# Block 2 of a two-block network on one Trainium2 core: the last twelve projections take their PSUM tiles from the buffers of the solve's and scan's tiles

## Chip, core and metric

The kernel runs on one core of a Trainium2 chip. The metric is the device time of one execution in microseconds, lower is better. TensorE (PE) multiplies matrices and writes its results to PSUM, a memory of eight banks; VectorE (DVE), ScalarE (ACT) and GpSimd (POOL) read them from there; SyncE (SP) issues most of the DMA transfers. TensorE's clock has two levels, 1.2 and 2.4 GHz, and the profile gives the granted share of the upper one (0.50 to 1.00).

## What is computed

The input is 512 tokens of width 1024. Block 1 is an RWKV-7 recurrence beside a neighbourhood attention, followed by a mixture of experts. Block 2, where the change lies, is a mixer of three branches and an MLP. All branches are fed by one projection of the normalised tokens:

```python
h = modulate(x, g, shift, scale)
z = h @ w_in
...
def gdn_chunk_scan(q, k, v, g, beta, s0):
    def step(s, xs):
        ...
        a = -jnp.einsum('bhid,bhjd->bhij', kb, kc) * jnp.exp(jnp.where(strict, diff, -jnp.inf))
        sol = lax.linalg.triangular_solve(eye - a, rhs, left_side=True, lower=True, unit_diagonal=True)
        w, u = sol[..., :dk], sol[..., dk:]
        v_new = u - w @ s
        o = (qc * jnp.exp(gcum)[..., None]) @ s + attn @ v_new
        s_new = jnp.exp(g_last)[..., None] * s + jnp.einsum('bhjd,bhje->bhde', kc * jnp.exp(g_last - gcum)[..., None], v_new)
        return s_new, o
```

Hyena takes a short convolution of its input (three taps) and then long convolutions; GLA and GDN gate their outputs with further columns of the projection. GDN has four heads, and runs forward and backward over the sequence.

## The kernel before

The program is written in Python as generators that emit instructions; a framework then orders the instructions of each engine by what they need, above all by when a buffer of a pool comes free. `weave` (L331) runs several generators together: it always advances the one whose emitted work divided by its weight is smallest.

**Projections.** `side_proj` (L1899) makes the 28 blocks of 128 columns that the mixer needs, one after the other. Each goes through `gemm_cm` (L297): a PSUM tile `gps` of 128x512, the weights loaded (`wraw`) and split into a rounded part `wh` on ScalarE (L287) and a rest `wl` on VectorE (L288), and 24 matmuls 128x512 in lines 293 to 295, eight steps of three products. What follows depends on the block: a short convolution (`conv`, L1277 and L1279) for the six `hy` blocks, tanh and a product (L1924, L1925) for the six `dg` and `gg` blocks. The result is stored to DRAM (L1926) for the later stages. The first 16 blocks are needed by GDN and GLA and are made by `early()` ahead of the branch of `gla_general` (L1689, L1690); the last twelve, `dg`/`gg` and `hy`, aren't needed until after the scan, and run beside `chain()`.

**The chain.** `chain()` solves two pairs of heads and then scans. `gdn_solve` (L1416) makes for each head the tiles `dps_` (L1427), `kkp` (L1437) and `qkp` (L1445), and calls `inverse` (L637) for the pair: 15 pairs of small steps on VectorE (L661, L662), a copy (L663) that goes to DRAM and back (`qd`, `qc`), a product on VectorE (L671, `qv`) and eight groups of products `ips` on TensorE (L682). `gdn_scan` (L1455) then goes through eight chunks. In each chunk the four heads have the small products `gxp` (L1467), `gup` (L1477), `gsp` (L1491) and `gop` (L1502, L1504), with steps on VectorE and ScalarE between them. The state runs from chunk to chunk.

**PSUM.** A tile of PSUM is taken by a tag, and each of the four tags `g`, `p`, `s` and `i` has two buffers. The projections run under a view that renames the tags:

```python
w = self.w = self.view(dict(p="g", s="g", i="p"), wg=512)
...
v = self.view({}, rib=2)
```

So a projection that asks for `g` gets `g`, and one that asked for `i` would get a buffer of `p`. The chain runs under `v`, which renames nothing: `dps_`, `kkp`, `qkp` and `gop` are on `p`, `gxp` and `gup` on `s`, `ips` and `gsp` on `i`. Before the change the projections thus have the two buffers of `g` for themselves. Tiles of one tag follow each other in the order in which the program asks for them: each waits until the readers of the tile two places earlier are done.

Of the kernel before, what the change touches and what calls it, by code (L numbers as in the profile page):

```python
# [19 lines left out]
T = 512  # L20
# [86 lines left out]
def w2_cols():  # L107

    r = {}
    ar = lambda a, n: np.arange(a, a + n)  # L110
    G, N = 768, 1952
    for hp in range(2):
        kv = np.concatenate([ar(N + 384 + 192 * hp, 192), ar(N + 768 + 192 * hp, 192)])
        for j in range(3):
            r[f"kv{hp}{j}"] = kv[128 * j:128 * j + 128]
    z = lambda n: np.full(n, -1)
    r["misc"] = np.concatenate([ar(N + 1536, 16), z(16), ar(G + 1152, 16), z(16), ar(G + 1168, 16), z(48)])
    for j in range(3):
        r[f"dq{j}"] = ar(N + 128 * j, 128)
    for hp in range(2):  # L120
        for nm, o in (("gk", 192), ("gq", 0)):
            r[f"{nm}{hp}"] = np.concatenate([ar(G + o + 96 * hp, 48), z(16), ar(G + o + 96 * hp + 48, 48), z(16)])
    for j in range(3):
        r[f"gv{j}"] = ar(G + 384 + 128 * j, 128)
        r[f"gg{j}"] = ar(G + 768 + 128 * j, 128)
        r[f"dg{j}"] = ar(N + 1152 + 128 * j, 128)
    for j in range(6):
        r[f"hy{j}"] = ar(128 * j, 128)
    return r
# [17 lines left out]
W2 = {n: i for i, n in enumerate(w2_cols())}  # L147
# [41 lines left out]
class K:  # L189
# [1709 lines left out]
    def side_proj(self, pool, later):  # L1899


        nc, A = self.nc, self.A
        cw = self.cp.tile([128, 6, 4], F32, name="hcw")
        nc.sync.dma_start(cw, A["hy_cw"])
        for n in SIDE_BLOCKS:
            self.we = nc.gpsimd if n in GDN_BLOCKS else nc.vector
            if n == "gk0":
                pool = later()
            ps = self.proj2(n, 128, T)
            if n in GDN_BLOCKS:  # L1910
                i = GDN_BLOCKS.index(n)
                y, d = self.conv_silu(pool, ps, 128, 8, 64, self.cw[:, (i + 6) % 9]), self.cvd[i]
            else:
                y = pool.tile([128, T], F32, name="sg", bufs=2)
                if n in self.gpd:
                    d = self.gpd[n]
                    nc.scalar.activation(y, ps, AF.Copy)
                elif n[:2] == "hy":
                    j = int(n[2])
                    d = self.hud[j]  # L1920
                    self.conv(pool, ps, 128, 8, 64, 3, cw[:, j], bias=cw[:, j, 3:4], out=y)
                else:
                    d = self.sgd[3 * (n[0] == "g") + int(n[2])]
                    nc.scalar.activation(y, ps, AF.Tanh, scale=0.5)  # L1924
                    nc.vector.scalar_tensor_tensor(y, y, 1.0, ps, op0=OP.add, op1=OP.mult)  # L1925
            nc.sync.dma_start(d, y)  # L1926
            self.there.add(n)
            yield 6
# [168 lines left out]
    def mixer_in(self):  # L2097

        nc, A, tc = self.nc, self.A, self.tc
        tp = tc.tile_pool  # L2100
        w, sp = self.w, self.w.sp

        def load(pool, d, tag):
            t = pool.tile([128, T], F32, name=tag, tag=tag, bufs=2)
            nc.sync.dma_start(t, d)
            return t

        with tp(name="mf", bufs=1) as mf:
            with tp(name="gd", bufs=1) as gd:
                w.misc(mf, 8)  # L2110
                v = self.view({}, rib=2)
                v.mfb = w.mfb

                st = {}
                w.there = set()
                def later():
                    w.spx.close()
                    return self.far.enter_context(tp(name="sp2", bufs=1, side="right"))
                side = w.side_proj(sp, later)

                def prep():
                    with tp(name="gt", bufs=1) as gt:
                        def src(n):
                            while n not in w.there:
                                next(side)
                            return load(gt, self.cvd[GDN_BLOCKS.index(n)], "yld")
                        st["g"] = v.gdn_gates(gd, v.mfb[:16], 8)
                        yield 10
                        st["q"] = yield from v.gdn_q(8, gd, gt, src)
                        for hp in range(2):  # L2130
                            st[hp] = yield from v.gdn_kv(hp, 8, gd, gt, src, hp)

                def early():
                    while not w.there.issuperset(SIDE_BLOCKS[:16]):
                        yield next(side)
                with tp(name="gf", bufs=1) as gf:
                    self.run(self.weave((early(), 96), (prep(), 60), (v.gla_flags(8, gf), 20)))
                with tp(name="gz", bufs=1) as ga:
                    v.gla_general(8, ga, lambda n: load(ga, self.gpd[n], "lsc"), self.oad)

                with tp(name="gs", bufs=1) as gs, tp(name="rp2", bufs=1) as v.rp:
                    heads = []

                    def chain():
                        with tp(name="gs2", bufs=1) as tmp, tp(name="ri2", bufs=1) as v.ri:
                            for hp in range(2):
                                kv, kT = st[hp]
                                E, TQ = yield from v.gdn_solve(hp, 8, gs, tmp, st["g"], kT, st["q"], hp)
                                heads.extend((2 * hp + e, kT[:, e], st["q"][:, 2 * hp + e], kv[:, :, e], kv[:, :, 2 + e], E[:, e], TQ[e])
                                             for e in range(2))  # L2150
                        yield from v.gdn_scan(8, gs, heads, st["g"], self.ogd)
                    next(side)
                    self.run(self.weave((chain(), 192), (side, 66)))
                    self.far.close()
                    self.oa = self.ox.enter_context(tp(name="oa", bufs=1, side="right")).tile([128, 8, 384], F32, name="oa")
                    nc.sync.dma_start(self.oa, self.oad.rearrange("c p d -> p c d"))
                    hp = self.far.enter_context(tp(name="hy", bufs=1, side="right"))
                    u = self.view(dict(p="g", s="g", i="g"))

                    def hyena():  # L2160
                        yield from u.hy_tables(hp)
                        yield from u.hyena(hp, 0)
                        yield from u.hyena(hp, 1)
            with tp(name="ga", bufs=1) as ga, tp(name="hn", bufs=1) as hn:
                un = self.view(dict(p="i"))
                self.run(self.weave((v.gla(8, False, ga, lambda n: load(ga, self.gpd[n], "lsc"), self.oa), 112),
                                    (un.head_norm_out(hn, self.ogd, 0, self.gng, 5), 36), (hyena(), 88)))
            self.far.close()
# [130 lines left out]
```

## Time and profile before

| | |
|---|---|
| runs | 2195.75, 2176.99, 2178.66 us; median 2178.66 |
| profiled execution | 2177.16 us, span 2175.4 us |
| mean granted clock | 0.932 |
| PE busy | 1954.9 us (90% of the span) |
| DVE busy | 1136.3 us (52%) |
| ACT busy | 719.2 us (33%) |
| POOL busy | 245.5 us (11%) |

All times inside the program are counted from the start of the span of the profiled execution. Matmuls are pipelined, so that the time from one's start to the next one's start is shorter than its own duration. Some matmul records are missing from a trace. A busy TensorE is not one at its peak: its granted clock says at which level it worked. The stretch that the change touches lies between 1390 and 1720 us: the last part of `early()`, the branch of `gla_general` (not taken), the solve with its two inverses, the scan, and the stage of Hyena and the gated norms behind it.

### The profile page before, as it was taken

The page shows a single profiled execution, that of the slowest core. Times are in us where ns is not written, and L with a number is a line of the kernel's source. Part 1 is how long each engine was busy: PE and PEld are TensorE (multiplying, and loading weights), DVE is VectorE, ACT ScalarE, POOL GpSimd, SP SyncE. Part 2 cuts the span into 40 slices and gives each one's busy share as a digit, 9 for nine tenths or more (in the row PEclk, how much of TensorE's full clock was granted, in tenths as well). Part 3 has the DMA queues.
Part 4 walks back from the last instruction along what each step waited for, and adds up shares of the span by engine and source line. Part 5 has one row for each costly group of instructions (what it writes and reads, how often), then busy time and mean ns, then how long its engine had stood idle before and what let it go on. Part 6 is the DMA issues. An engine that isn't in the chain of part 4 may idle for free. (4 is left out here: it accounts for less than half of the span.)

```text
span 2175.4 us, 37783 instructions
## 1 busy us (share of the span) xinstructions
PE 1954.9 (90%) x15280; PEld 1427.1 (66%) x15280; DVE 1136.3 (52%) x2542; ACT 719.2 (33%) x1390; POOL 245.5 (11%) x254
## 2 busy tenths in 40 slices
PE   7899999999698889988999487899999789999997
PEld 6676767666466764444524266677667577898897
DVE  4565645563362545455461487487456675434433
ACT  4333223333262433121322365422153234312321
POOL 0101011110100211111000031130002150010000
PEclk9999989999799989999999798999579899999999
DMA  6424232432854549979687433332152342333332
GB/s 160 145 61 131 82 102 65 126 111 75 183 175 158 165 133 322 327 262 328 244 300 251 181 116 103 104 81 80 44 171 62 127 144 76 97 93 93 97 92 74
DMA packets 177123, 312.21 MB, mean 144 GB/s; under 512 B 78648, under 2 KB 95816, under 8 KB 176938
## 3 DMA queue, kind: packets, MB, share of 16 engines
q1 hardware_dynamic: 167274, 291.84, 42.6%
q0 software_dynamic: 6784, 10.51, 1.7%
q10 hardware_dynamic: 2880, 7.34, 1.1%
q8 instruction: 123, 2.02, 0.4%
q14 instruction: 62, 0.51, 0.1%
HBM read 278.23 MB, written 39.77 MB: 146 GB/s over the span
## 5 line engine op out<-in xcount | busy, mean ns | idle before, releaser
L288 DVE TENSOR_TENSOR wl<-wraw,wh 128x1024 fp32r<-128x1024 f32 (+2 forms) x215 | 227.9, 1062 | 235.7 <-ACT wh L287 235.3
L287 ACT ACTIVATE wh<-wraw 128x512 fp32r<-128x512 f32 (+2 forms) x233 | 195.7, 844 | 251.7 <-PE gpt L326 136.9
L293 PE MATMUL gps<-hh,wh 128*128 128x512 f32 x568 | 235.2, 415 | 0.4 <-DVE kS L380 0.4
L294 PE MATMUL gps<-hh,wl 128*128 128x512 f32 x568 | 232.5, 410 | 1.2 <-DVE wl L288 1.2
L295 PE MATMUL gps<-hl,wh 128*128 128x512 f32 x568 | 233.0, 411 | 0.0
L1178 PE MATMUL hps<-w,xT 128*64 128x512 f32 x512 | 142.4, 611 | 3.3 <-DMA w<-in_w_moe 3.2
L324 PE MATMUL gpt<-wh,mh 128*128 128x256 f32 x512 | 142.9, 279 | 0.0
L325 PE MATMUL gpt<-wl,mh 128*128 128x256 f32 x512 | 142.9, 279 | 0.0
L326 PE MATMUL gpt<-wh,ml 128*128 128x256 f32 x512 | 142.9, 279 | 0.0
L293 PEld LDWEIGHTS gps<-hh,wh 128*128 128x128 f32 x568 | 108.2, 191 | 29.5 <-issue 2.9
L294 PEld LDWEIGHTS gps<-hh,wl 128*128 128x128 f32 x568 | 107.9, 190 | 29.5 <-DVE wl L288 4.2
L295 PEld LDWEIGHTS gps<-hl,wh 128*128 128x128 f32 x568 | 107.7, 190 | 25.7 <-issue 2.0
L293 PE MATMUL gps<-lhh,wh 128*128 128x512 f32 x232 | 98.0, 424 | 16.7 <-ACT wh L287 6.2
L294 PE MATMUL gps<-lhh,wl 128*128 128x512 f32 x232 | 96.2, 416 | 3.8 <-DVE wl L288 2.2
L324 PEld LDWEIGHTS gpt<-wh,mh 128*128 128x128 f32 x512 | 96.2, 188 | 0.1
L325 PEld LDWEIGHTS gpt<-wl,mh 128*128 128x128 f32 x512 | 96.2, 188 | 0.1
L326 PEld LDWEIGHTS gpt<-wh,ml 128*128 128x128 f32 x512 | 96.2, 188 | 0.0
L295 PE MATMUL gps<-lhl,wh 128*128 128x512 f32 x232 | 95.4, 413 | 0.0
L2003 POOL TENSOR_TENSOR x<-x,xev 128x512 f32<-128x512 f32 x36 | 50.2, 1403 | 388.3 <-DVE xev L2001 388.0
L1178 PEld LDWEIGHTS hps<-w,xT 128*64 128x64 f32 x512 | 36.9, 138 | 66.2 <-issue 50.8
L1279 DVE SCALAR_TENSOR_TENSOR cout<-cpad,cw,cout 128x512 f32<-128x512 f32 (+1 forms) x90 | 66.9, 743 | 2.1
L2019 DVE TENSOR_TENSOR uld<-uld 128x512 f32<-128x512 f32 x32 | 22.2, 693 | 87.3 <-ACT uld L2018 87.3
(1181 smaller groups left out, 4226.9 us busy)
## 6 DMA issues: line engine op xcount, KB each, us to landing
w<-in_w_moe SPq DMA_DIRECT2D x192, 512.0 KB
wraw<-in_w_modb SPq DMA_DIRECT2D x48, 512.0 KB
wraw<-in_w_in_2b SPq DMA_DIRECT2D x41, 512.0 KB
wraw<-in_w_mlp1b SPq DMA_DIRECT2D x32, 512.0 KB
wraw<-in_w_mlp2b SPq DMA_DIRECT2D x32, 512.0 KB
wraw<-in_w_inb SPq DMA_DIRECT2D x31, 512.0 KB
bm<-in_c_bias SPq DMA_DIRECT2D x16, 256.0 KB
wraw<-in_w_inb ACTq DMA_DIRECT2D x8, 512.0 KB
```

The source lines that it names most:

```text
L287: nc.scalar.activation(wh, raw[:, o:o + g], AF.Copy)
L288: self.we.tensor_sub(wl, raw[:, o:o + g], wh)
L293: nc.tensor.matmul(ps, wh, hh, start=first, stop=False)
L294: nc.tensor.matmul(ps, wl, hh, start=False, stop=False)
L295: nc.tensor.matmul(ps, wh, hl, start=False, stop=last)
L324: nc.tensor.matmul(ps, hh[:, g, sl], wh[:, k], start=f, stop=False, skip_group_check=True)
L325: nc.tensor.matmul(ps, hh[:, g, sl], wl[:, k], start=False, stop=False, skip_group_check=True)
L326: nc.tensor.matmul(ps, hl[:, g, sl], wh[:, k], start=False, stop=l, skip_group_check=True)
L1178: nc.tensor.matmul(ps[q], xT[:, 4 * kh + k, q], self.parts[h][:, 512 * (k - 2 * c):512 * (k - 2 * c) + 512], start=kh == 0 and k == 0, sto ...
L1279: nc.vector.scalar_tensor_tensor(ov[:n], pv[:n, :, j:j + L], wcol[:n, j:j + 1], ov[:n], op0=OP.mult, op1=OP.add)
L2003: (nc.gpsimd if last is None or cb < 3 else nc.vector).tensor_add(o, o, t)
L2019: nc.vector.tensor_mul(f, f, f)
```

## The change

The seventeenth and later projections take their PSUM tile by tag `i`, which the view makes `p`: the two buffers of `dps_`, `kkp`, `qkp` and `gop`. The seventeenth projection is no longer emitted ahead of the chain, and the weight of the projections in the weave is 72 instead of 66 (the chain's is 192).

```diff
@@ side_proj
-            ps = self.proj2(n, 128, T)
+            ps = self.gemm_cm("w_in_2b", W2.get(n, n), self.hh, self.hl, T, tag="i" if len(self.there) >= 16 else "g")
@@ mixer_in
-                    next(side)
-                    self.run(self.weave((chain(), 192), (side, 66)))
+                    self.run(self.weave((chain(), 192), (side, 72)))
```

The order of TensorE's instructions changes from the branch of `gla_general` to the end of the scan. Of the twelve projections, 33 matmuls stood ahead of the branch before and none do now. Between the branch and the first inverse's `ips` there were 107; now there are 114. Here is TensorE from the last groups of the first inverse on, before the change (`gps` is a projection, one number for each):

```order
L682 MATMUL ips_13819<-W_13798,Z_13722 64x64 x16
L295 MATMUL gps_14242<-lhl_11436,wh_14261 128x512
L293 MATMUL gps_14242<-lhh_11435,wh_14261 128x512
L294 MATMUL gps_14242<-lhh_11435,wl_14262 128x512
L295 MATMUL gps_14242<-lhl_11436,wh_14261 128x512
L1477 MATMUL gup_14281<-gX_14221,TQ0_13817 64x96 x2
L1477 MATMUL gup_14288<-gX_14227,TQ1_13836 64x96 x2
L1502 MATMUL gop_14338<-gS_7764,qT__12153 64x96 x2
L1502 MATMUL gop_14345<-gS_7764,qT__12153 64x96 x2
L293 MATMUL gps_14391<-lhh_11435,wh_14394 128x512
```

After that row 119 further matmuls of five projections follow before the second inverse's `ips`. The same place in the changed kernel:

```order
L1477 MATMUL gup_14249<-gX_14227,TQ1_13836 64x96 x2
L1502 MATMUL gop_14299<-gS_7764,qT__12153 64x96 x2
L1502 MATMUL gop_14306<-gS_7764,qT__12153 64x96 x2
L1504 MATMUL gop_14299<-vn__14247,E0_13421 64x96 x2
L1504 MATMUL gop_14306<-vn__14254,E0_13421 64x96 x2
L1502 MATMUL gop_14313<-gS_7764,qT__12153 64x96 x2
L1502 MATMUL gop_14320<-gS_7764,qT__12153 64x96 x2
L682 MATMUL ips_14025<-qv_14022,No_13970 64x64 x16
L682 MATMUL ips_14044<-qv_14022,No_13974 64x64 x16
```

The second inverse's products now follow the first chunk's groups at once: the next projection's tile shares `p` with the `gop` tiles of heads 2 and 3 (14313, 14320), which need the second inverse.

On VectorE, the small steps of the second inverse (`tmp16`, `q16`) before the change, with convolution (`sg`) and weight split (`wl`) between them:

```order
L662 TENSOR_REDUCE q16_14023<-tmp16_14024 128x8
L1277 TENSOR_SCALAR sg_14608<-cpad_14609,hcw_11604 128x512
L661 SCALAR_TENSOR_TENSOR tmp16_14024<-q16_14023,n16_14021 128x9x9
L1279 SCALAR_TENSOR_TENSOR sg_14608<-cpad_14609,hcw_11604,sg_14608 128x512
L662 TENSOR_REDUCE q16_14023<-tmp16_14024 128x9
L1279 SCALAR_TENSOR_TENSOR sg_14608<-cpad_14609,hcw_11604,sg_14608 128x512
L661 SCALAR_TENSOR_TENSOR tmp16_14024<-q16_14023,n16_14021 128x10x10
L288 TENSOR_TENSOR wl_14747<-wraw_14728,wh_14746 128x512
L662 TENSOR_REDUCE q16_14023<-tmp16_14024 128x10
L288 TENSOR_TENSOR wl_14885<-wraw_14882,wh_14884 128x512
```

And in the changed kernel:

```order
L662 TENSOR_REDUCE q16_13984<-tmp16_13985 128x8
L661 SCALAR_TENSOR_TENSOR tmp16_13985<-q16_13984,n16_13982 128x9x9
L662 TENSOR_REDUCE q16_13984<-tmp16_13985 128x9
L661 SCALAR_TENSOR_TENSOR tmp16_13985<-q16_13984,n16_13982 128x10x10
L662 TENSOR_REDUCE q16_13984<-tmp16_13985 128x10
L661 SCALAR_TENSOR_TENSOR tmp16_13985<-q16_13984,n16_13982 128x11x11
```

The 15 pairs of steps now follow one another with nothing between them; the convolutions and splits stand in the scan's chunks instead.

In the scan, TensorE before the change, in chunk 1 (the one projection there, `gps_15217`, is strung through chunks 0 to 3, and chunks 4 to 7 hold none):

```order
L293 MATMUL gps_15217<-lhh_11435,wh_15220 128x512
L1477 MATMUL gup_14435<-gX_14370,TQ0_13817 64x96 x2
L294 MATMUL gps_15217<-lhh_11435,wl_15221 128x512
L295 MATMUL gps_15217<-lhl_11436,wh_15220 128x512
L1477 MATMUL gup_14442<-gX_14376,TQ1_13836 64x96 x2
L1491 MATMUL gsp_14463<-vd__14438,kv0_12336 96x96
L1491 MATMUL gsp_14464<-vd__14438,kv0_12336 96x96
L1477 MATMUL gup_14449<-gX_14382,TQ2_14195 64x96 x2
```

And in the changed kernel, in chunk 4:

```order
L1467 MATMUL gxp_14847<-gSn_14752,kT1_12839 64x96 x2
L293 MATMUL gps_14909<-lhh_11435,wh_14912 128x512
L1477 MATMUL gup_14853<-gX_14832,TQ0_13817 64x96 x2
L294 MATMUL gps_14909<-lhh_11435,wl_14913 128x512
L295 MATMUL gps_14909<-lhl_11436,wh_14912 128x512
L1477 MATMUL gup_14860<-gX_14838,TQ1_13836 64x96 x2
L1491 MATMUL gsp_14881<-vd__14856,kv0_12336 96x96
L1491 MATMUL gsp_14882<-vd__14856,kv0_12336 96x96
L1477 MATMUL gup_14867<-gX_14844,TQ2_14195 64x96 x2
L293 MATMUL gps_14909<-lhh_11435,wh_14912 128x512
```

The scan now holds seven projections: one in chunk 1 (three single matmuls and a run of 21), one in chunk 2 as a run of 24, two in chunk 3 (a run of 24, and one strung out), and one in each of chunks 4, 5 and 6, strung out as here. Chunk 7 holds none.

## Rows read from the trace of the kernel before

**Rows 1.** Windows by stage: busy time and instructions of each engine, granted clock, DMA share.
```profile
1410.00:1505.50 95.50, 88.46 (x1057) 70.30 (x1059) 73.15 (x151) 23.07 (x42) 20.88 (x23) 0.98 0.35 90
1505.50:1599.00 93.50, 91.08 (x602) 58.14 (x600) 46.83 (x176) 19.55 (x61) 0.00 (x0) 0.59 0.14 46
```

**Rows 2.** Chain that ended last, in the scan: start, duration, what.
```profile
1557.34 1.00 PE gup L1477 x8
...
1558.92 0.51 PE gup L1477 x4
...
1568.97 1.00 PE gup L1477 x8
```

**Rows 3.** Timeline of PE in chunk 1 of the scan, at the full clock.
```profile
1512.63 0.49 PE L295 MATMUL gps<-lhl,wh 128*128 128x512 f32 x1
1513.05 0.39 PE L1467 MATMUL gxp<-gSn,kT 96*64 96x96 f32 x4
1513.37 0.50 PE L293 MATMUL gps<-lhh,wh 128*128 128x512 f32 x1
...
1514.26 0.39 PE L1467 MATMUL gxp<-gSn,kT 96*64 96x96 f32 x4
```

**Rows 4.** Windows, all engines; the third figure from the end is PE's clock.
```profile
1410.00:1413.00 3.00, 2.65 (x5) 1.49 (x5) 0.39 (x2) 0.63 (x1) 0.00 (x0) 0.50 0.03 8
1413.00:1418.00 5.00, 5.00 (x75) 3.92 (x75) 3.94 (x6) 0.60 (x1) 2.30 (x2) 0.93 0.00 2
1517.50:1522.00 4.50, 4.50 (x36) 3.04 (x36) 2.35 (x10) 1.24 (x5) 0.00 (x0) 1.00 0.02 4
1522.00:1526.00 4.00, 4.00 (x21) 2.48 (x23) 1.48 (x6) 0.34 (x1) 0.00 (x0) 0.62 0.13 49
1526.00:1588.00 62.00, 62.00 (x386) 39.70 (x384) 29.15 (x113) 12.44 (x39) 0.00 (x0) 0.50 0.12 39
```

**Rows 5.** Windows of the tile gps alone (PE, PEld, DVE, ACT), by stretch.
```profile
508.00:518.00 10.00, 6.42 (x18) 2.85 (x18) 0.00 (x0) 0.69 (x1) 1.00 0.15 39
1421.50:1427.20 5.70, 5.70 (x24) 4.42 (x24) 0.00 (x0) 0.00 (x0) 1.00 0.47 110
1461.00:1496.70 35.70, 30.41 (x124) 22.81 (x124) 0.68 (x1) 3.29 (x6) 1.00 0.47 119
1508.00:1522.00 14.00, 3.77 (x10) 1.53 (x9) 0.00 (x0) 0.00 (x0) 1.00 0.04 15
1526.00:1545.00 19.00, 5.25 (x8) 2.19 (x8) 0.00 (x0) 0.36 (x1) 0.50 0.00 1
```

**Rows 6.** Timeline of PE at the second inverse's products.
```profile
1496.72 2.08 PE L682 MATMUL ips<-qv,No 64*64 64x64 f32 x64 [0.40 <-DVE qv L671]
```

**Rows 7.** Timeline of PE around the branch.
```profile
1399.90 2.32 PE L1381 MATMUL tcp<-ct,kv 128*96 128x128 f32 x8 [1.06 <-DVE kv L1372]
...
1410.35 0.79 PE L293 MATMUL gps<-lhh,wh 128*128 128x512 f32 x1 [5.87 <-DVE q L658]
1410.94 0.63 PE L294 MATMUL gps<-lhh,wl 128*128 128x512 f32 x1
1411.37 0.63 PE L295 MATMUL gps<-lhl,wh 128*128 128x512 f32 x1
```

**Rows 8.** Timeline of DVE ahead of the branch, one of three such splits.
```profile
1390.45 0.69 DVE L288 TENSOR_TENSOR wl<-wraw,wh 128x512 fp32r<-128x512 f32 x1 [0.31 <-ACT wh L287]
```

**Rows 9.** DVE groups by line, 1471.6 to 1487.3; then two rows of its timeline.
```profile
L1279 DVE SCALAR_TENSOR_TENSOR sg<-cpad,hcw,sg 128x512 f32<-128x512 f32 x6 | 4.5, 748 | 0.0
...
L288 DVE TENSOR_TENSOR wl<-wraw,wh 128x512 fp32r<-128x512 f32 x4 | 2.7, 687 | 0.0
L1277 DVE TENSOR_SCALAR sg<-cpad,hcw 128x512 f32<-128x512 f32 x3 | 1.6, 543 | 0.1
...
1487.30 0.37 DVE L663 COPY q<-q 128x256 f32<-128x256 f32 x1
...
1495.35 1.23 DVE L671 TENSOR_TENSOR qv<-qc,ct 128x1024 f32<-128x1024 f32 x1 [0.19 <-DMA qc<-qd]
```

## The prediction

> **What bounds the kernel now.** I first cut the part of the span that the change touches into stages [rows 1]. In the solve, 1410 to 1505.5, TensorE is busy 88.46 of 95.5 us at a clock of 0.98. In the scan, 1505.5 to 1599, it is busy 91.08 of 93.5 us, but its granted clock is 0.59, while VectorE has 46.83 us of work. So TensorE is full in both, and the odd stage is the scan, most of which runs at the lower of the clock's two levels.
>
> The chain of waits shows that stage as TensorE alone, group behind group [rows 2]: a chunk begins with the group of eight `gup` at 1557.34 and the next at 1568.97, 11.6 us apart, and a group of four in between takes 0.51 us (1558.92). At the full clock such a group is followed after 0.32 us (1513.05 to 1513.37) [rows 3]. The granted clock [rows 4] is 1.00 until 1522, falls after the few projection matmuls there have become rarer, is 0.62 to 1526 and 0.50, the lower level, to 1588. In the RWKV scan of block 1, where 18 projection matmuls lie in 10 us [rows 5], it stays at 1.00; here 10 lie in the 14 us before it falls, and 8 in 19 us in which it does not come back.
>
> The solve is bound otherwise: by the steps of `inverse` on VectorE. TensorE fills the wait with projections, 124 recorded matmuls in 35.7 us [rows 5], and waits only 0.40 us for the inverse's first product at 1496.72 [rows 6].
>
> **The change, part by part.** Twelve projections of 24 matmuls keep their work. What changes is where they stand: before, 33 matmuls ahead of the branch, then four and a half projections up to the first inverse, five between the two inverses, one in the scan; after, none ahead of the branch, five up to the first inverse, none between the inverses, seven in the scan. A block of 24 takes 5.70 us at the full clock [rows 5].
>
> *Ahead of the branch.* TensorE comes back from the branch at 1410.35 after 5.87 us. What the branch waits for is the chain of k and v, whose last transposes are among the matmuls there and, at 1399.90, waited 1.06 us for VectorE, not for the projections [rows 7]. So 33 matmuls × 0.24 = 7.8 us of TensorE are not 7.8 us gained. What that chain loses to them is splits: three `wl` of 0.69 us on VectorE after 1390, 2.1 us [rows 8]. Bounds 0 and −4; I take −2.
>
> *Resume to the first inverse.* TensorE returns at half clock: 0.50 from 1410 to 1413, 0.93 from 1413 [rows 4]. Now three projection matmuls stand ahead of the first `dps_` (1.4 us). After the change that `dps_` goes first, and a whole block of 24 follows before the second `dps_`, where 12 stood. Twelve more are 2.9 us, or 5.2 at the spacing of 0.43 us that matmuls have at the half clock (1410.94 to 1411.37) [rows 7], less 1.4: between +1.5 and +4. Set against it, VectorE has the second head's steps waiting either way (−2 at best). I take +2.
>
> *Second inverse.* In 1471.6 to 1487.3 VectorE runs the inverse's 30 small steps, but also four `wl` and nine passes of the short convolution, 4.5 + 2.7 + 1.6 = 8.8 us [rows 9]. After the change its row there is bare. Passes overlap by some 0.1 us each, so 13 × 0.6 = 8 us is the most that can go; some of the small steps wait for each other all the same, and I take 6. The copy to DRAM and back (1487.30 to 1495.35, 8 us) [rows 9] shares its queue with a weight load and two stores; another −1. Together −7 (−4 to −9). The price: TensorE has nothing for some 26 us (35.7 less the relief and the six matmuls and few small groups left there). Idle for the branch, it came back at 0.50 [rows 4]; so the inverse's products, which take from 1496.72 [rows 6] to the end of the stage at 1505.5, 8.8 us, start at the half clock. If that holds throughout they take twice as long at most, +9; if it returns halfway, +4. I take +4.
>
> *Scan.* A chunk without projections at the full clock: 11.6 × 0.32/0.51 = 7.3 us [rows 2, 3]. A projection adds 5.7 us in one piece. Scattered it adds more: a single matmul among small groups costs 0.42 us (1512.63 to 1513.05), a run of three 0.89 (1513.37 to 1514.26) [rows 3]. The new order gives runs of 3, 1, 2, 4, 1, 1, 1, 1, 1, 9 in each of chunks 4 to 6: 0.9 + 6 × 0.42 + 0.65 + 1.1 + 2.2 = 7.3 us, with 0.23 for each further matmul of a run. So: rest of chunk 0, 3.3; chunk 1 with three singles and 21 in a row, 13.6; chunk 2 with a block, 13.0; chunk 3 with a block and a scattered projection, 20.3; chunks 4 to 6, 14.6 each, 43.8; chunk 7 with the tail, 9.7 (estimates for the ends, from the same rates). The sum is 103.7 us at the full clock, against 93.5 now: +10. What is gained by the clock is spent on six more projections. Between the blocks of chunks 1 to 3 lie stretches of some 7 us without any; the clock held for 4.5 us of such (1517.5 to 1522) and fell in the next 4 [rows 4]. Each such chunk at the half clock costs 11.6 − 7.3 = 4.3; of three I count one, +4 (0 to +13). Chunks 4 to 6 have 24 projection matmuls in 14.6 us, about the 18 in 10 of the RWKV scan, so I count them at the full clock.
>
> *Shared buffers and the stage behind.* The two buffers now hold projections and the tiles of solve and scan in turn, so a projection's first matmul can wait for a chain step to read its tile, and a chain step for a projection's convolution to read its tile. At the full clock the scan's TensorE is busy 4.50 of 4.50 us with the buffers apart [rows 4], so there is little wait to start from; I count 0 (0 to +5). In the stage behind, the same work is ordered otherwise: 0 ± 5.
>
> About this the Trainium skill, "TensorE: Matmul & The Clock Gate", section "A second HAM failure mode: psum-queue depth-cycling", speaks against the change: cycling PSUM through one queue gave the engine short idles between groups, and the clock then swung between its levels. No row of this case shows that swing; by it the second rival's price below would be the likelier one.
>
> **Sum.** −2 + 2 − 7 + 4 + 10 + 4 = +11 us on the profiled execution's 2177.16 (span 2175.4), so 2188.2; the median of the runs is 2178.66, 1.5 above that execution, and the lowest 2176.99. I forecast **2188**: slightly slower, which is inside the 1% (21.8 us) that a measurement of this kernel can tell from no change.
>
> **Rivals.**
> *The clock stays high and the blocks fill waits (faster).* If chunk 3's and the fine chunks' scattered matmuls cost no more than a block (5.7 instead of 7.3: −6.4), no stretch falls to the half clock (−4), and the inverse's products keep the clock (−4), the sum is −3; with −4 instead of −2 ahead of the branch and the relief at its end of −9, −7: 2170. With another 5 us from the next stage it is 2165. For it: the clock of 1.00 in the RWKV scan. Against: TensorE's total work does not shrink, and its only slack, the branch and the 26 us, grows. To pass −1% (2157) more would be needed than any row offers.
>
> *The scan stays at the half clock (slower).* After 26 us of idling the clock is at 0.50 when chunk 0 resumes. If the projections, strung between small groups, do not lift it, a chunk costs 11.6 us plus 24 × 0.43 = 10.3, about 22 without any extra for scattering; seven projections cost 72 us where the one now there took some 10 in the scan. Then −2 + 2 − 7 + 9 + 62 = +64: 2241. If it holds only up to the block of chunk 3, that is three projections, (3 × 4.6 + 2 × 4.3 + 9 − 4) on top of the forecast, 27: about 2215. It decides on whether 24 matmuls in a chunk are enough. For it: 8 in 19 us did not bring the clock back; against it: 0.93 from 1413 on, some 3 us after the branch [rows 4], when solve and projections came together, and the RWKV scan.
>
> *It does not hold the projections back.* If buffers came free so early that the order stayed the same, nothing would happen, 2178. The order of the changed kernel excludes it: seven projections stand in the scan.
>
> *Gain and loss cancel.* The clock's gain pays for the projections and the relief of VectorE is lost to idling: 2175 to 2182. That is the forecast's mechanism with smaller terms.
>
> **How the numbers follow.** Forecast, with its cancelling variant, 0.70; the faster rival 0.14, of which 0.08 lies beyond −1%, for a gain that I can't price; the half clock through the first chunks or all the scan 0.16, nearly all beyond +1%, to which 0.05 comes from the forecast's own upper end (resume +2, inverse +5, more half-clock stretches +9, buffers +5: 2209). So faster 0.08, same 0.72, slower 0.20. The range runs from the faster rival with a helpful next stage, 2165, to 2215, the forecast's upper end and the partial half-clock case; what is left out is the whole scan at half clock and the last of the gains.
>
> **What would show it.** Right: the granted clock in the scan above 0.9 from chunk 4 on; a scan of about 107 us in place of 93.5; TensorE idle some 25 us before the second inverse's products, and those at first at half speed; VectorE's steps of the second inverse bare and some 6 us shorter. Wrong: a scan clock near 0.5 with chunks of 20 us and more (second rival), or a scan under 95 us (first). Were TensorE to stand still inside the scan in front of projection matmuls or behind convolutions, the shared buffers would be the term that I set at nothing.

## The result, and the profile after

| | before | after |
|---|---|---|
| median | 2181.26 us (2176.99 to 2195.75, 4 runs) | 2216.64 us (2204.26 to 2226.26, 4 runs) |
| ratio | | 1.0144, 95% interval 1.0098 to 1.019 |
| profiled execution's span, mean clock | 2175.4 us, 0.932 | 2215.9 us, 0.926 |

The change makes the kernel 1.4% slower. That is 31 us on the kernel before, where the forecast was 11. On the median that the prediction started from, the ratio gives 2178.66 × 1.0144 = 2210, inside the range near its upper end. The median after by itself, 2216.64, lies 1.6 us above that end: the range was met narrowly.

Single executions of one kernel differ by more than most terms of the sum: 33 runs of the kernel before on the chip of the later experiments lay between 2163 and 2196 us. Part of that arises long before the change's place. The last instruction that all kernels here have in common ahead of the branch is a small product, L1679: it starts at 1373.36 us before and at 1380.41 after, 7.05 us later, although nothing ahead of it differs. So the traces are compared by stages, from one landmark to the next. The landmarks are that product; VectorE's return from the branch (L1425); TensorE's products of the first and of the second inverse (`ips`); the last `gop` of the scan; and the last step at L1890 in the stage behind. The products of the first inverse, 8.0 us in every kernel, are left out. Where the order of two kernels is the same or nearly so, their traces agree: before, e3, e5, e7 and e8 differ by at most 0.4 us in the first two columns. The last column is the sum of all differences behind L1679. Stage lengths in us, from the timelines:

| kernel | L1679 to return | return to first `ips` | between the `ips` | second `ips` | scan | stage behind | sum against before |
|---|---|---|---|---|---|---|---|
| before | 35.08 | 44.69 | 35.58 | 8.81 | 93.44 | 115.86 | |
| after | 31.99 | 50.02 | 27.12 | 10.11 | 121.10 | 126.48 | +33.4 |
| e1, tag alone | 31.95 | 59.99 | 26.98 | 10.26 | 132.37 | 126.55 | +55.6 |
| e2, weight alone | 36.16 | 46.97 | 38.32 | 7.95 | 94.91 | 115.51 | +6.4 |
| e3, last six share | 34.84 | 44.70 | 27.38 | 9.54 | 135.02 | 126.35 | +44.3 |
| e4, even | 32.07 | 48.10 | 26.28 | 9.74 | 101.44 | 124.19 | +8.4 |
| e5, last one held | 35.17 | 44.53 | 35.68 | 8.81 | 93.65 | 125.96 | +10.3 |
| e6, even and early | 31.98 | 49.80 | 30.07 | 10.34 | 105.75 | 117.99 | +12.5 |
| e7, even, last four | 34.96 | 44.89 | 34.24 | 9.42 | 98.18 | 118.35 | +6.7 |
| e8, even, last three | 35.01 | 44.92 | 35.56 | 10.26 | 96.55 | 117.22 | +6.1 |

Two stages carry the loss: the scan, +27.7, and the stage behind it, +10.6.

The stores of the scan's chunks (`ogd`, on SyncE's queue) in the kernel after show the chunks. The columns are start, duration, what:

```profile
1511.90 0.33 SPq L1507 DMA_DIRECT2D ogd<-Og  x1
1530.52 0.32 SPq L1507 DMA_DIRECT2D ogd<-Og  x1
1550.82 0.32 SPq L1507 DMA_DIRECT2D ogd<-Og  x1
1573.06 0.32 SPq L1507 DMA_DIRECT2D ogd<-Og  x1
1591.22 0.32 SPq L1507 DMA_DIRECT2D ogd<-Og  x1
1606.40 0.32 SPq L1507 DMA_DIRECT2D ogd<-Og  x1
1623.15 0.32 SPq L1507 DMA_DIRECT2D ogd<-Og  x1
1629.46 0.33 SPq L1507 DMA_DIRECT2D ogd<-Og  x1
```

Chunks 1 to 6 take 18.6, 20.3, 22.2, 18.2, 15.2 and 16.8 us; the prediction had 13.6, 13.0, 20.3 and three times 14.6. Why they are longer is in the windows of the same stretch. The third figure from the end is the granted clock, the first pair behind the length is TensorE; these answer to [rows 1, 4]. The last two lie in chunks 4 and 6:

```profile
1412.40:1507.60 95.20, 65.06 (x946) 53.38 (x948) 59.06 (x128) 14.55 (x27) 20.48 (x14) 0.82 0.24 59
1507.60:1628.80 121.20, 116.62 (x747) 75.42 (x744) 61.60 (x203) 30.12 (x78) 0.74 (x10) 0.86 0.18 60
```
```profile
1512.00:1517.00 5.00, 5.00 (x14) 3.40 (x15) 1.33 (x5) 0.00 (x0) 0.00 (x0) 0.57 0.10 39
1517.00:1522.00 5.00, 5.00 (x20) 3.70 (x21) 0.69 (x1) 0.67 (x2) 0.00 (x0) 0.74 0.00 0
1522.00:1527.00 5.00, 4.62 (x56) 3.06 (x54) 4.10 (x16) 2.87 (x8) 0.00 (x0) 1.00 0.15 54
1527.00:1532.00 5.00, 4.98 (x32) 3.42 (x32) 3.13 (x12) 0.84 (x3) 0.00 (x0) 0.78 0.37 102
...
1547.00:1552.00 5.00, 5.00 (x18) 3.37 (x18) 1.43 (x6) 0.34 (x1) 0.00 (x0) 0.50 0.08 29
1552.00:1557.00 5.00, 5.00 (x20) 4.04 (x19) 0.69 (x1) 0.64 (x1) 0.00 (x0) 0.83 0.04 14
...
1582.00:1587.00 5.00, 5.00 (x17) 3.28 (x18) 0.31 (x1) 0.48 (x1) 0.00 (x0) 0.50 0.00 0
...
1615.10:1617.60 2.50, 2.50 (x7) 2.04 (x7) 0.31 (x1) 0.00 (x0) 0.00 (x0) 0.50 0.00 0
```

The clock swings. In chunks 1 to 3 it falls in a stretch with no projections or single ones, or as the next block begins, and comes back only within that block. So the block pays as well. It also falls once in chunk 4 and once in chunk 6, among strung projections, though not in chunk 5, whose order is the same (0.50 from 1581.0 and from 1615.4; 1.00 from 1591.2 to 1606.4), and at the end of chunk 7. This is TensorE's timeline in the block of chunk 1, whose matmuls start 0.43 us apart up to 1519.34 and 0.23 us apart from 1519.67:

```profile
1517.63 0.63 PE L294 MATMUL gps<-lhh,wl 128*128 128x512 f32 x1
1518.06 0.63 PE L295 MATMUL gps<-lhl,wh 128*128 128x512 f32 x1
...
1519.67 0.40 PE L293 MATMUL gps<-lhh,wh 128*128 128x512 f32 x1
1519.91 0.40 PE L294 MATMUL gps<-lhh,wl 128*128 128x512 f32 x1
```

TensorE hardly stands still meanwhile: over the scan it waits 4.6 of 121.2 us. Part of that lies ahead of a fall (it is busy 3.63 of the 5.40 us from 1537.6 to 1543, and the clock falls at about 1543), so this trace alone does not rule idle time out as the cause. The kernel before does for its own fall: TensorE is busy 17.27 of 17.27 us from the scan's start to 1522.8, and the clock falls there all the same [rows 4]. So does e3 below.

The second inverse went as forecast. On VectorE its steps start at 1480.64 and end with the copy at 1489.74, 9.1 us where it was 15.7, with no pass and no split left among them. TensorE waited for it:

```profile
1497.55 3.68 PE L682 MATMUL ips<-qv,No 64*64 64x64 f32 x64 [19.39 <-DVE qv L671]
```

Its row of before is [rows 6]. The 64 matmuls take 3.68 us instead of 2.08, so they do start at the half clock; the last 128 take 4.02 us, as before. Between the inverses TensorE is busy 4.79 of 27.12 us: it waits 22 us, where the prediction had 26.

Behind the scan, in the timeline of TensorE:

```profile
1628.17 0.59 PE L1504 MATMUL gop<-vn__15341,E 64*64 64x96 f32 x4
1634.26 1.94 PE L1298 MATMUL ttp<-ct,cfb 128*128 128x128 f32 x8 [5.51 <-DVE cfb L1287]
...
1651.09 0.38 PE L1858 MATMUL hyt<-ct,hv 128*128 128x128 f32 x2
```

and of SyncE's queue:

```profile
1642.55 2.04 SPq L1848 DMA_DIRECT2D hv<-hud  x2
```

Hyena's input `hv` is loaded 14 us after the last `gop`. Before, the same load left 3.9 us ahead of the scan's end, and its first product (`hyt`) came 0.6 us behind the end (from the queue and from TensorE's timeline):

```profile
1595.03 0.94 SPq L1848 DMA_DIRECT2D hv<-hud  x2
1599.57 1.08 PE L1858 MATMUL hyt<-ct,hv 128*128 128x128 f32 x4 [0.61 <-DMA hv<-hud]
```

Now TensorE waits 5.51 us, works for a while at the half clock on GLA's products, and comes to Hyena 22.3 us behind the scan's end.

### The profile page after: what moved, and what is told of

Read it like the earlier page. It is cut to its first block, busy times and chain, and to the rows that moved or that the text cites. A ratio compares the mean times of both kernels' runs of the same rounds, so it can differ in the third digit from the quotient of the medians.

```text
span 2215.9 us, 37768 instructions
## 1 busy us (share of the span) xinstructions
PE 1962.7 (89%) x15280; PEld 1433.8 (65%) x15280; DVE 1133.4 (51%) x2542; ACT 721.2 (33%) x1390; POOL 246.0 (11%) x254
## 5 line engine op out<-in xcount | busy, mean ns | idle before, releaser
L295 PE MATMUL gps<-hl,wh 128*128 128x512 f32 x568 | 234.6, 414 | 0.0
L295 PEld LDWEIGHTS gps<-hl,wh 128*128 128x128 f32 x568 | 108.7, 192 | 25.9 <-issue 2.0
L295 PE MATMUL gps<-lhl,wh 128*128 128x512 f32 x232 | 97.6, 423 | 0.0
```

What stands on the lines that cost most here:

```text
L295: nc.tensor.matmul(ps, wh, hl, start=False, stop=last)
```

## The experiments

**Each half of the change by itself.** e1 is the change to the tag, with the issue ahead and the weight of 66 kept:

```diff
-            ps = self.proj2(n, 128, T)
+            ps = self.gemm_cm("w_in_2b", W2.get(n, n), self.hh, self.hl, T, tag="i" if len(self.there) >= 16 else "g")
```

> The tag alone: the last twelve projections take their PSUM tiles from the buffers of p, and the issue ahead of the chain and the weight of 66 stay. The order still holds no projection matmul ahead of the branch, 135 up to the first inverse, none between the inverses, and some six projections in the scan. Theory A (the late projections cost: the scan with a clock that swings, and the stage behind that starts late): as the change, +25 to +38 us on the kernel before. Rival B (the cost comes from the issue ahead and the weight): within 6 us of the kernel before.

Measured: 2238.02 us, ratio 1.0239 (1.0205 to 1.0274). Theory A's sign, but more than it allowed (52 us by the ratio): the tag alone costs more than the whole change, so the other half, beside it, takes some of the cost away. The table says where: 135 projection matmuls now stand ahead of the first inverse and the steps of the solve queue behind them (return to first `ips` 59.99 us, 10 more than after), and the scan has 132.37 us.

e2 is the other half, the tag left as it was:

```diff
-                    next(side)
-                    self.run(self.weave((chain(), 192), (side, 66)))
+                    self.run(self.weave((chain(), 192), (side, 72)))
```

> The other half alone: no issue ahead of the chain and the weight 72, the projections on their own buffers g. The order is nearly that of the kernel before: five projections between the inverses, one in the scan. Theory A: within 6 us of the kernel before. Rival B: +15 us or more.

Measured: 2194.2 us, ratio 1.0037 (1.0013 to 1.006). Rival B falls: this half costs 8 us by the ratio, a little more than the 6 that theory A allowed. By the stages it is 6.4: 1.1 up to the return, 2.3 up to the first inverse, 2.7 between the inverses, 1.5 in the scan, and −1.1 in the rest.

**Sharing for fewer.** e3 is e1 with a later threshold:

```diff
-            ps = self.proj2(n, 128, T)
+            ps = self.gemm_cm("w_in_2b", W2.get(n, n), self.hh, self.hl, T, tag="i" if len(self.there) >= 22 else "g")
```

> Only the last six projections share the buffers of p; the six before them keep g. Ahead of the branch and up to the first inverse the order is that of the kernel before, between the inverses stands none, in the scan about six. Theory A: nearly all of the cost is in the scan and behind it, so +20 to +33 us, with a relief of the second inverse of 6 to 9 us as in the change. Rival C (the cost comes from sharing in the solve, where projections stand between the steps of the first pair): +12 us or less.

Measured: 2226.75 us, ratio 1.0185 (1.0149 to 1.0222). The solve is that of before up to the first inverse (44.70 us; before 44.69), the second inverse is relieved by 8.2 us, and still the kernel is 40 us slower, more than theory A's upper end. Rival C falls: the cost is there without any sharing in the solve. The scan alone takes 135.02 us. Its windows show it at the half clock most of the time, and from 1524 to 1612 TensorE is busy 88.00 of 88.00 us while the clock rises and falls three times:

```profile
1502.50:1637.60 135.10, 132.62 (x722) 81.21 (x720) 60.72 (x200) 28.50 (x75) 0.74 (x10) 0.69 0.14 49
```
```profile
1524.00:1612.00 88.00, 88.00 (x406) 53.12 (x404) 35.80 (x117) 15.95 (x40) 0.44 (x6) 0.62 0.11 37
1550.00:1558.00 8.00, 8.00 (x38) 4.17 (x38) 3.19 (x12) 1.27 (x4) 0.00 (x0) 0.50 0.07 26
1558.00:1566.00 8.00, 8.00 (x41) 5.67 (x37) 3.18 (x8) 2.75 (x6) 0.00 (x0) 0.78 0.19 65
1566.00:1574.00 8.00, 8.00 (x51) 4.71 (x50) 4.77 (x19) 1.02 (x3) 0.15 (x2) 0.65 0.16 59
1591.78:1611.50 19.72, 19.72 (x59) 11.08 (x60) 5.79 (x19) 2.00 (x5) 0.00 (x0) 0.50 0.03 11
```

Its order has one run of 13 to 17 projection matmuls in each of chunks 1 to 4, with 6 to 12 others in ones, twos and threes. Chunk 5, the last row, has 25 in runs of one to six, and the clock stays at 0.50 for the first 19.7 of its 24.9 us: strung matmuls did not lift it there once it was down.

**The same work, strung evenly.** e4 is the whole change, with the last twelve projections given to the weave three matmuls at a time:

```diff
-            ps = self.proj2(n, 128, T)
+            tg = "i" if len(self.there) >= 16 else "g"
+            if len(self.there) < 16:
+                ps = self.proj2(n, 128, T)
+            else:
+                ps = self.ps.tile([128, 512], F32, name="gps", tag=tg, bufs=2)
+                k = 0
+                for wh, wl in self.wsplit(A["w_in_2b"][W2.get(n, n)].rearrange("p k c -> p (k c)"), 1024):
+                    wh, wl = [t.rearrange("p (k c) -> p k c", c=128) for t in (wh, wl)]
+                    for i in range(wh.shape[1]):
+                        self.mm3(ps, wh[:, i], wl[:, i], self.hh[:, k], self.hl[:, k], k == 0, k == 7)
+                        k += 1
+                        yield 0.75
...
-            yield 6
+            yield 6 if len(self.there) <= 16 else 0
...
-                    next(side)
-                    self.run(self.weave((chain(), 192), (side, 66)))
+                    self.run(self.weave((chain(), 192), (side, 72)))
```

> The change, but the last twelve projections are emitted three matmuls at a time, so that in the scan they are strung evenly through all chunks in runs of one to six (one run of 12, one of 9) instead of runs of 21 to 24 with stretches of 7 us without any. Theory A, by the swinging clock: the granted clock in the scan is above 0.95, chunks take some 15 us, the scan is 6 to 14 us shorter than in the change (122 us there), the whole 5 to 15 us faster than the change. Rival D (the projections wait for the shared buffers, or the switching between kinds costs as much as the clock): the scan is not shorter than 120 us, the whole within 4 us of the change or slower.

Measured: 2186.61 us, ratio 1.0027 (1.0001 to 1.0053). This is the decisive run. The scan holds the 168 projection matmuls that it holds in the change, on the same two buffers, and takes 101.44 us instead of 121.10. The whole is 30 us faster than the change by the medians and 25 by the stages, more than theory A expected, and rival D falls. The windows show the clock at its upper level from 1511 on, after some 10 us at the half clock early in the scan, and TensorE nearly without waits (the first window begins 1.3 us ahead of the scan):

```profile
1495.20:1598.00 102.80, 102.10 (x789) 63.02 (x784) 61.11 (x205) 30.16 (x79) 0.74 (x10) 0.95 0.16 52
```
```profile
1501.00:1510.50 9.50, 9.50 (x35) 5.35 (x33) 3.05 (x12) 0.63 (x1) 0.00 (x0) 0.51 0.06 21
1507.00:1520.00 13.00, 12.91 (x97) 7.74 (x96) 6.47 (x23) 4.01 (x10) 0.00 (x0) 0.83 0.06 22
1520.00:1533.00 13.00, 12.91 (x106) 7.95 (x102) 8.17 (x27) 4.26 (x11) 0.00 (x0) 1.00 0.18 63
1533.00:1546.00 13.00, 13.00 (x87) 8.35 (x85) 8.58 (x28) 3.58 (x9) 0.29 (x4) 1.00 0.20 69
...
1572.00:1585.00 13.00, 13.00 (x102) 7.93 (x101) 8.67 (x29) 4.07 (x11) 0.15 (x2) 1.00 0.10 37
```

Of the 19.7 us between the two scans some 12 are the clock's by an estimate from the mean clocks (0.14 of 121.1 us against 0.05 of 101.4, as if all of a scan's time went with the clock). Another 3.9 are waits: TensorE stands still for 4.5 us of the one and 0.6 of the other. The rest is not explained. So the run shows that the cost is in the order and not in the amount of work or the buffers; blocks and waits change together in it.

**The stage behind, alone.** e5 lets only the very last projection share:

```diff
-            ps = self.proj2(n, 128, T)
+            ps = self.gemm_cm("w_in_2b", W2.get(n, n), self.hh, self.hl, T, tag="i" if len(self.there) >= 27 else "g")
```

> Only the very last projection shares the buffers of p. Ahead of the scan the order is that of the kernel before; the one projection that stood in chunks 0 to 3 of the scan now stands in chunks 5 to 7. Theory A, its term for the stage behind (a projection that ends with the scan keeps its pools, so that Hyena's first loads and products start late): solve and second inverse within 1 us of the kernel before, scan within 4 us, Hyena's first product 15 to 26 us after the scan's end instead of 0.6 us, the whole +5 to +11 us. Rival E (the stage behind only reorders, TensorE has other work there): within 3 us of the kernel before.

Measured: 2194.3 us, ratio 1.0059 (1.0037 to 1.0082). Solve, inverses and scan are those of before within 0.3 us in every column of the table, and the stage behind takes 125.96 us instead of 115.86: +10.1. Rival E falls. The whole is +12.9 us by the ratio and +10.3 by the stages, where theory A had 5 to 11. In TensorE's timeline:

```profile
1605.52 0.59 PE L1504 MATMUL gop<-vn__15341,E 64*64 64x96 f32 x4
1611.30 1.94 PE L1298 MATMUL ttp<-ct,cfb 128*128 128x128 f32 x8 [5.19 <-DVE cfb L1287]
...
1629.35 0.38 PE L1858 MATMUL hyt<-ct,hv 128*128 128x128 f32 x2
```

It is the picture of the change: some 5 us of waiting, and Hyena more than 20 us behind the scan. What SyncE's queue waits for says more. The first load of the stage, `oa`, leaves only after a projection product (L295) in both kernels, for which it waited 17.5 us here and 12.2 in the kernel after; the first load of Hyena's tables, `hraw`, waits 3.0 us for the store of the last projection. These rows are from the kernel after:

```profile
SPq L2155 <- PE gps L295: 12.2, 1, 12.2
SPq L1818 <- DMA hud<-sg: 3.0, 1, 3.0
```

By then the loads of GLA and of the norms (`lsc`, `ls`, `hsg`, `hO`) stand ahead of `hv` in that queue; before, `hv` stood ahead of them.

**Even, and done earlier.** e6 is e4 with another weight, so that the last projection ends in chunk 5. Against e4:

```diff
-                    self.run(self.weave((chain(), 192), (side, 72)))
+                    self.run(self.weave((chain(), 192), (side, 84)))
```

> As the even kernel, with the weight 84 instead of 72, so that the last projection ends in chunk 5 and 33 projection matmuls stand between the inverses. Theory A: scan and solve as in the even kernel within 5 us (chunks 6 and 7 without projections fall to the half clock), the stage behind at most 2 us longer than in the kernel before instead of 8, so the whole 3 to 9 us faster than the even kernel, within 5 us of the kernel before. Rival E (the stage behind is not what costs): as the even kernel, +6 us on the kernel before.

Measured: 2190.63 us, ratio 1.0042 (1.0018 to 1.0065). The stage behind is 117.99 us, 2.1 above that of before instead of 8.3, and Hyena's first product comes at the scan's end again. So that term hangs on when the last projection ends. The whole is not faster than e4 all the same, so theory A's 3 to 9 us miss: more work before the first `ips` (+1.7), 3.8 us less relief between the inverses, +0.6 in the products of the second and +4.3 in the scan, whose mean clock is 0.88, take it back.

**Fewer in the scan.** e7 keeps the issue ahead, lets only the last four share and be strung, and has the weight 80; e8 is the same with 25 for 24, the last three. Against e4:

```diff
-            tg = "i" if len(self.there) >= 16 else "g"
-            if len(self.there) < 16:
+            tg = "i" if len(self.there) >= 24 else "g"
+            if len(self.there) < 24:
...
-            yield 6 if len(self.there) <= 16 else 0
+            yield 6 if len(self.there) <= 24 else 0
...
-                    self.run(self.weave((chain(), 192), (side, 72)))
+                    next(side)
+                    self.run(self.weave((chain(), 192), (side, 80)))
```

> Only the last four projections share p and are emitted three matmuls at a time, the weight is 80 and the issue ahead stays: ahead of the first inverse 111 projection matmuls (107 before), between the inverses some 45 (123 before), in chunks 1 to 5 of the scan some 90, evenly strung. Theory A: second inverse 4 to 7 us earlier, scan 91 to 96 us, stage behind 0 to +2, so 2 to 9 us faster than the kernel before. Rival D (strung projections cost in the scan what they save between the inverses): within 2 us, or slower.

> As the kernel of the last four, with the last three: between the inverses some 70 projection matmuls, in chunks 3 to 5 of the scan some 65. Theory A: second inverse 2 to 5 us earlier, scan 90 to 95 us, stage behind 0 to +2, the whole 0 to 7 us faster than the kernel before. Rival D: within 2 us, or slower.

Measured: e7 2192.81 us, ratio 1.0039 (1.0014 to 1.0064); e8 2189.43 us, 1.0035 (1.0012 to 1.0058). Both are slower than the kernel before, so theory A's numbers miss here, and rival D is right in its numbers for these two. The relief that I counted on is nearly absent: between the `ips` 34.24 and 35.56 us, against 35.58 before. The scans, 98.18 and 96.55 us, are above what theory A gave too; e7's has a mean clock of 0.79. VectorE's groups in e7 between 1474 and 1490 us say why the relief is missing; six passes of the convolution and three splits still stand among the inverse's steps or just ahead of them:

```profile
L1279 DVE SCALAR_TENSOR_TENSOR sg<-cpad,hcw,sg 128x512 f32<-128x512 f32 x4 | 3.0, 744 | 0.0
L288 DVE TENSOR_TENSOR wl<-wraw,wh 128x512 fp32r<-128x512 f32 x3 | 2.1, 685 | 1.2 <-ACT wh L287 1.2
L1277 DVE TENSOR_SCALAR sg<-cpad,hcw 128x512 f32<-128x512 f32 x2 | 1.1, 542 | 3.5 <-ACT cpad L1270 3.5
```

The steps from first to copy take 14.4 us there (1476.09 to 1490.49) and 9.1 in e4 (1469.87 to 1478.97). No kernel tried is faster than the one before.

## Why the prediction was right, and where its sizes were off

- **Ahead of the branch**, −2 forecast: −3.1, and not the 7.8 us of TensorE, as argued. Of it 2.6 lie behind the step `kv` (L1372): 9.05 us from its start to the return before, 6.45 after. A split, a product (L1925) and five projection matmuls stood there; which of them it was is not shown.
- **Resume to the first inverse**, +2: +5.3. The second `dps_` starts 14.9 us behind the return instead of 10.1, which is nearly all of it: a whole block of 24 stands ahead of it, and I had priced twelve matmuls.
- **Second inverse**, −7: −8.5. The mechanism was as said, and TensorE waited 22 us for 26: the steps take 6.6 us less, and the copy to DRAM and back 6.4 us instead of 8. e7 and e8 show that the relief is one of VectorE's queue: what must be gone are the passes, and with two or three projections left between the inverses nearly nothing is gained.
- **Its products at the half clock**, +4: +1.3. The clock was back before the last 128.
- **Scan at the full clock**, +10: near. The kernel after has 121.1 us at a mean clock of 0.86, which would be 104.1 at the full clock (an estimate, as if all of the time went with the clock), against 103.7. No run has this order at the full clock; e4, in another order and at a mean of 0.95, takes 101.44.
- **Half clock in the scan**, +4: this is the step that failed in size. The scan took 121.1 us, so the term is 17.4, above even its upper end of 13. I had seen that the clock falls in a stretch of 7 us without projections, and charged it to the small groups of one chunk of three. The trace shows the half clock in chunks 1, 2 and 3, and that the block behind the stretch runs 6 to 12 of its matmuls at it, which I had priced at the full clock. It also shows it in chunks 4 and 6, which I had counted at the full clock because of the RWKV scan: from chunk 4 on the mean is 0.88, not above 0.9. e4, with the blocks strung out, has 1.00 from 1511 to the scan's end.
- **Stage behind**, 0 ± 5: +10.6. I had looked at the work, which is the same, and not at what releases it. e5 moves nothing but one projection and costs 10.1 there; e6 ends the projections earlier and has 2.1. That it is the memory of the projections' pools, which Hyena's take over when the last projection ends, was argued from the code and fits with the waits of the loads `oa` and `hraw` shown with e5; it was not tested apart from that end.
- **Shared buffers**, 0: right for the scan. In the kernel after, TensorE stands still in front of projection products for a reader of `gop` for 0.5 us in all, and e4 on the same two buffers has it busy 100.80 of 101.44 us. In the solve the table of e1 points to another cost of sharing, that of order: projections that follow in line stand in front of the chain's steps.

The sum was +11 and the trace's +33.4: of the 22.4 between them the scan is 13.7 (27.7 where 14 stood) and the stage behind 10.6, and the other terms together −1.9. That the time still fell into the range is in part luck: its upper end was built from the half clock up to chunk 3 and from other terms, and the stage behind, which brought 10.6, stood in it with 0. More than 1% slower, as it came out, had a chance of 0.20. The rule in the Trainium skill, "TensorE: Matmul & The Clock Gate", section "A second HAM failure mode: psum-queue depth-cycling", was right in its result, a clock that swings between its levels, which I had given too little weight. Its cause there, short idles of the engine, is not needed here: the clock fell in the kernel before with TensorE busy 17.27 of 17.27 us, and three times in e3 within 88.00 of 88.00, and e4 with the same PSUM buffers holds 1.00 for 87 us. In the kernel after, short waits do stand ahead of some falls, and what part they have there is open.

## What to carry to other kernels

Where a chain of small matmuls lets TensorE's clock fall, it counts how the filler matmuls are spread, and not only how many there are: in blocks, the clock fell between them here, and the block that followed paid too; strung evenly in e4, the same matmuls held it. That is no guarantee: strung ones did not hold it in chunks 4 and 6 of the changed kernel, nor lift it in chunk 5 of e3, so look at the granted clock of each stretch. Before work is moved later, see what starts when it ends: one projection moved from the scan's beginning to its end cost 10 us behind the scan, with the stages ahead unchanged. Work that looks free beside a waiting engine can sit in the queue of the engine that is waited for; what counts is whether all of it leaves that queue.

## What the runs showed of the hardware

The granted clock fell from 1.00 to 0.50 while TensorE was busy without a gap in a run of small matmuls: in the kernel before, after 17.27 of 17.27 us, and three times in e3 within 88.00 of 88.00 us. In chunks 1 to 3 of the kernel after it rose in the middle of a run of large ones. At 0.50 large matmuls followed each other after 0.43 us, at 1.00 after 0.23. With the large matmuls strung among the small ones, the clock stayed at 1.00 for 87 us (1511 to 1598 in e4); in e3 a chunk with 25 strung ones stayed at 0.50 for 19.7 us.
